# Attention stage of a two-layer hybrid backbone: weight splits in parts, low parts and LayerNorm sums on another engine, mean copied out of PSUM, other buffers for the MLP's input

## The chip, the cores and the metric

The kernel runs on one core of one Trainium2 chip. The metric is the device time of one execution in microseconds (us); the time of a kernel is the median of several executions. Engines are called PE (TensorE, with PEld for its weight loads), DVE (VectorE), ACT (ScalarE), POOL (GpSimd) and SP (SyncE, which here only issues DMAs).

## What is computed

Two post-norm layers over 1024 latent tokens and 256 context tokens of width 1024, all in float32. Layer 0 is retention and gated linear attention; layer 1, where the change lies, is windowed grouped-query attention in which latent queries also read all context keys. Cut to what matters here (the head axes, masks and modulation are in words):

```
h   = modulate(x)                               # shift and scale by SiLU(c)
q, k, v = split(h @ w_qkv)                      # 16 query heads, 4 KV heads, width 64, 2-D rotary on q and k
s   = q @ k.T / 8                               # keys: own block of 128 and its two neighbours (+-128), and 256 context keys
m   = max(s, sink[head]);  e = exp(s - m)
y   = (e @ v) / (sum(e) + exp(sink - m))        # learned sink logit for each head
x   = layer_norm(alpha * x + gate * (y @ w_out))
h   = modulate(x)
x   = layer_norm(alpha * x + gate2 * (square(relu(h @ w1)) @ w2))
```

`layer_norm` takes mean and variance over the 1024 channels of a token, then multiplies by g and adds b.

## The kernel before, in words

Activations lie transposed: channels on partitions (8 tiles of 128, `KT`), tokens on columns. A matmul in full precision is done in three: each float32 operand is split into a high part (a cast to the reduced type `F32R`) and a low part (the value less its high part), and `mm3` multiplies high with high, high with low and low with high. So every weight and every activation that enters such a matmul costs a cast and a subtraction on another engine.

The attention stage works on 32 groups: for each block n of 128 queries (0 to 7), each of four KV heads g, with the four query heads that share it. For a group:

- `scores(i)`, i from 0 to 3: the scores of one query head in a PSUM tile `pS` (two of them in turn), their maximum (L1400, DVE), the exponent's bias (L1401, DVE), the exponential into a tile `E` (L1404, ACT; seven buffers of 640 columns under the tag "E").
- `dens()`: the denominators, and `dg` (L1417, POOL), four diagonal tiles that carry their reciprocals.
- `turn(kk)`, five for a block inside (four in the first and the last block): four PE transposes of `E` into a PSUM bank `pE` (two in turn, L65), copied to `Et` by ACT (L1429), for kk = 2 by DVE (L1427).
- `pv(kk)`: the product with the values into `pO`. `end()`: the denominators' product, `yf` (L1448, L1449, DVE), its high part `yh` (L1451, ACT) and its low part `yl` (L1452, DVE).
- `qt`, the queries, come by two DMAs of POOL's queue (L1380) for every second group; two such tiles are used in turn.

The code weaves the groups: the scores of the next group are issued between the transposes of the present one. Into this weave it hangs, in small steps, the work on tokens whose attention is done, 256 at a time:

- `w_load` and `w_prep` bring one 128x1024 tile of the output weight for each group from the seventh on: DMA, high part by ACT (L1333), low part by `en` (L1334), which is POOL, but DVE for four of the last eight tiles.
- `residual` runs `w_out_steps`: for each of 8 output tiles 24 matmuls into the single PSUM bank `pW`, in two halves, then gate and addition (L758, DVE). The last residual has no group beside it and takes the two `pE` banks. Two of the residuals end with `make_h`, which makes the MLP's input from 256 tokens that are normalised already: `hf` by ACT (L378), its high part by DVE (L259), its low part by DVE and POOL in turn (L260, the list `los`). Here `hf` lies in the tag "ln_q", with one buffer.
- `norm` runs `layer_norm_steps` with `pe_sums` False: the eight channel tiles are added on DVE (L701, L703) into `sm` (named `ln_s` in rows), one matmul with ones turns that sum into the mean in `pW`, DVE subtracts it from PSUM (L712, 512 columns at a time), ACT squares (L714, tag "ln_q", one buffer), DVE adds the squares (L721), a second matmul gives the variance, then square root, reciprocal (L725), multiplication (L730, DVE) and g, b (L736, POOL). Three of these LayerNorms lie in the stage and what follows it; a fourth is made by other code on PE.

Behind the last group the last residual's remaining tiles and the third LayerNorm run by themselves, and then the MLP begins: its first matmuls (`k`, then squared ReLU from L1046 on) need `hf` split, its weights are split by L251 (ACT) and L252 (POOL).

What sets the order: PE's instructions in the groups are chained in the order of the code (`TE.kept`). On the other engines the scheduler of the framework sets the order at build time; each engine then takes its instructions strictly in that order. POOL's queue holds its arithmetic and its DMAs in one order.

Of the kernel before, what the change touches and what calls it, by code (L numbers as in the profile page):

```python
# [34 lines left out]
def backbone(ctx: ExitStack, tc: tile.TileContext, xT, cin, wmod, bmod, lng, lnb, w1, w2,  # L35
# [330 lines left out]

    def make_h(src, l, idx, j, hh, hl, tp, tag, nb=1, hi_eng=None):
        for _ in h_steps(src, l, idx, j, hh, hl, tp, tag, nb, hi_eng):
            pass

    def h_steps(src, l, idx, j, hh, hl, tp, tag, nb=1, hi_eng=None, los=(V, G)):

        n = src.shape[2]
        for k2 in range(KT // 2):
            tmp = tp.tile([P, 2, 256], F32, tag=tag, name=nm("hf"), bufs=nb)
            for i in range(2):
# [298 lines left out]

    def layer_norm_steps(acc, l, s, tp, ts, tq, nb, pe_sums, pL, qn=1024, tail=None):

# [20 lines left out]
        if pe_sums:  # L698
            part(pp, acc, 0, 4)
        else:  # L700
            V.tensor_tensor(sm[:, 0, :], acc[:, 0, :], acc[:, 1, :], ALU.add)  # L701
            for k in range(2, KT):
                V.tensor_tensor(sm[:, 0, :], sm[:, 0, :], acc[:, k, :], ALU.add)  # L703
                if k == 4:
                    yield
        yield
        pm = mean(pp, 0)
        pp = pL() if pe_sums else None
        st_ = qn // n
        for k0 in range(0, KT, st_):  # L710
# [4 lines left out]
            if pe_sums:  # L715
                part(pp, sq, k0 // 2, (k0 + st_) // 2)
            else:
                for i in range(st_):
                    if k0 + i == 0:
                        continue  # L720
                    V.tensor_tensor(sm[:, 1, :], sq[:, 0, :] if k0 + i == 1 else sm[:, 1, :], sq[:, i, :], ALU.add)  # L721
            yield
# [581 lines left out]
    with pool(name="p2", bufs=1) as p2:  # L1304
# [24 lines left out]
        def w_prep():  # L1329
            if raws:  # L1330
                raw, en = raws.pop(0)
                both = wg.tile([P, 2, 1024], F32R, tag="w", name=nm("w"))
                S.copy(both[:, 0, :], raw)  # L1333
                en.tensor_tensor(both[:, 1, :], raw, both[:, 0, :].bitcast(F32), ALU.subtract)  # L1334
                ready.append((both[:, 0, :], both[:, 1, :]))

        def residual(y, t, ci):
# [8 lines left out]
            if t in (NT - 3, NT - 1):  # L1346
                make_h(accs[1][:, :, o0:o0 + 256], 1, 1, 0, *[y_[:, :, o0:o0 + 256] for y_ in yall], p2, "ln_q", 1)

        def norm(t, ci):

            o0 = (t - 1) * P - CH[ci][0]
            TE.kept = False
            for _ in layer_norm_steps(accs[ci][:, :, o0:o0 + 256], 1, 0, p2, "ln_s", "ln_q", 1, False, pW, 512):
                yield
# [6 lines left out]
        def group(n, g):  # L1361
# [80 lines left out]
            def end():  # L1442
# [8 lines left out]
                S.copy(ysl, yf)  # L1451
                V.tensor_tensor(yall[1][:, 2 * g:2 * g + 2, lt:lt + P], yf, ysl.bitcast(F32), ALU.subtract)  # L1452

# [180 lines left out]
```

## Time and profile before

| | us |
|---|---|
| three executions | 3015.12, 3013.77, 3008.65; median 3013.77 |
| the profiled execution, its own time | 3020.45 |
| its span in the trace | 3018.6 |
| attention stage in the trace (groups) | 1847 to 2230 |
| last residual, LayerNorm, MLP's first input | 2222 to 2282 |

The mean granted clock of PE in the profiled execution is 0.979. In the rows a group of instructions reads: line, engine, operation, output<-input, partitions x elements, xcount | busy time in us, mean ns of one | idle time of the engine ahead of them, and what ended it. A row of the timeline reads: start in us, duration in us, engine, line, operation, tiles, and in brackets how long the engine was idle ahead of it and what released it. A row of waits reads: engine, tile and line that waited, what released it; us in all, number, longest.

### The profile page before, as it was taken

The page shows a single profiled execution, that of the slowest core. Times are in us where ns is not written, and L with a number is a line of the kernel's source. Part 1 is how long each engine was busy: PE and PEld are TensorE (multiplying, and loading weights), DVE is VectorE, ACT ScalarE, POOL GpSimd, SP SyncE. Part 2 cuts the span into 40 slices and gives each one's busy share as a digit, 9 for nine tenths or more (in the row PEclk, how much of TensorE's full clock was granted, in tenths as well). Part 3 has the DMA queues.
Part 4 walks back from the last instruction along what each step waited for, and adds up shares of the span by engine and source line. Part 5 has one row for each costly group of instructions (what it writes and reads, how often), then busy time and mean ns, then how long its engine had stood idle before and what let it go on. Part 6 is the DMA issues. An engine that isn't in the chain of part 4 may idle for free. (4 is left out here: it accounts for less than half of the span.)

```text
span 3018.6 us, 42215 instructions
## 1 busy us (share of the span) xinstructions
PE 2863.4 (95%) x17204; PEld 2403.4 (80%) x17204; DVE 1662.4 (55%) x2709; ACT 978.9 (32%) x1628; POOL 808.1 (27%) x610
## 2 busy tenths in 40 slices
PE   7989998999999999999999999898888999999997
PEld 4866788888888888888888777677677888888886
DVE  3754477777755544445434645677775343433345
ACT  4433344444221211111112623555553221122113
POOL 3120145545211111111111511333353222122111
PEclk9999999999999999999999999999999999999999
DMA  7377575663221221222200483221221111111111
GB/s 254 112 233 243 183 263 187 203 203 109 67 73 57 81 70 60 77 68 76 70 29 8 134 223 92 66 88 58 78 98 36 56 56 42 43 56 53 37 37 57
DMA packets 168353, 304.44 MB, mean 101 GB/s; under 512 B 13504, under 2 KB 98752, under 8 KB 167648
## 3 DMA queue, kind: packets, MB, share of 16 engines
q1 hardware_dynamic: 149744, 272.91, 27.7%
q0 software_dynamic: 6480, 16.26, 2.1%
q10 hardware_dynamic: 11936, 12.59, 1.5%
q8 instruction: 135, 2.21, 0.3%
q14 instruction: 58, 0.48, 0.0%
HBM read 257.67 MB, written 44.04 MB: 100 GB/s over the span
## 5 line engine op out<-in xcount | busy, mean ns | idle before, releaser
L252 POOL TENSOR_TENSOR w<-raw,w 128x1024 fp32r<-128x1024 f32 x182 | 439.4, 2423 | 1518.2 <-ACT w L251 1457.9
L62 PE MATMUL k<-hh,w 128*128 128x256 f32 (+1 forms) x3264 | 824.6, 338 | 5.3 <-DVE hh L259 3.4
L62 PE MATMUL k<-uh,w 128*128 128x512 f32 (+1 forms) x2816 | 764.4, 352 | 8.1 <-DVE acc L1064 7.7
L1064 DVE SCALAR_TENSOR_TENSOR acc<-k,gta,acc 128x512 f32<-128x512 f32 (+1 forms) x704 | 440.8, 648 | 565.7 <-PE k L62 564.0
L62 PEld LDWEIGHTS k<-hh,w 128*128 128x128 f32 x3264 | 567.6, 191 | 83.0 <-issue 12.9
L62 PEld LDWEIGHTS k<-uh,w 128*128 128x128 f32 x2816 | 501.4, 189 | 89.2 <-DVE acc L1064 15.4
L62 PE MATMUL k<-hl,w 128*128 128x256 f32 (+1 forms) x1632 | 553.1, 339 | 5.8 <-POOL hl L260 4.5
L62 PE MATMUL k<-ul,w 128*128 128x512 f32 (+1 forms) x1408 | 494.8, 351 | 0.0
L251 ACT CAST w<-raw 128x1024 fp32r<-128x1024 f32 x228 | 235.8, 1047 | 694.2 <-PE k L62 471.5
L62 PEld LDWEIGHTS k<-hl,w 128*128 128x128 f32 x1632 | 311.4, 191 | 45.4 <-POOL hl L260 5.9
L62 PEld LDWEIGHTS k<-ul,w 128*128 128x128 f32 x1408 | 266.1, 189 | 36.5 <-issue 1.2
L62 PE MATMUL k<-yh,w 128*128 128x256 f32 (+1 forms) x1088 | 271.9, 336 | 21.2 <-DVE acc L758 11.2
L1046 ACT ACTIVATE r<-k 128x512 f32<-128x512 f32 (+1 forms) x176 | 90.7, 516 | 613.1 <-PE k L62 610.9
L62 PEld LDWEIGHTS k<-yh,w 128*128 128x128 f32 x1088 | 192.6, 196 | 42.8 <-DVE acc L758 12.6
L181 DVE SCALAR_TENSOR_TENSOR k<-raw,cs,k 128x256 f32<-128x256 f32 (+1 forms) x168 | 96.5, 574 | 159.5 <-DMA raw<-in_wmod 157.4
L62 PE MATMUL k<-yl,w 128*128 128x256 f32 (+1 forms) x544 | 181.5, 334 | 0.0
L1049 DVE TENSOR_TENSOR r<-r 128x1024 f32<-128x1024 f32 (+1 forms) x88 | 110.6, 1257 | 72.0 <-ACT uh L1048 71.8
L62 PE MATMUL pS<-kall,qt 128*128 128x256 f32 (+1 forms) x512 | 124.5, 355 | 13.8 <-ACT E L1404 13.3
L736 POOL TENSOR_SCALAR acc<-acc,lg_t,lb_t 128x256 f32<-128x256 f32 x124 | 102.3, 839 | 103.0 <-DVE acc L730 56.8
L1404 ACT ACTIVATE E<-pS,sm 128x640 f32<-128x640 f32 (+1 forms) x128 | 98.7, 771 | 77.1 <-DVE sm L1401 75.0
L1400 DVE TENSOR_REDUCE sm<-pS 128x1 f32<-128x640 f32 (+1 forms) x128 | 100.4, 786 | 36.1 <-PE pS L62 33.5
L65 PE MATMUL pE<-ident,E 128*128 128x128 f32 x608 | 96.5, 284 | 21.1 <-DVE Et L1427 20.1
(279 smaller groups left out, 3862.9 us busy)
## 6 DMA issues: line engine op xcount, KB each, us to landing
raw<-in_w SPq DMA_DIRECT2D x128, 512.0 KB, 3.3
raw<-in_wo SPq DMA_DIRECT2D x72, 512.0 KB, 3.4
raw<-in_wmod SPq DMA_DIRECT2D x128, 256.0 KB, 2.7
raw<-in_wfm SPq DMA_DIRECT2D x48, 512.0 KB, 5.2
raw<-in_wmod SPq DMA_DIRECT2D x32, 512.0 KB, 4.4
kt<-kd SPq DMA_DIRECT2D x20, 512.0 KB, 5.5
qt<-qT POOLq DMA_DIRECT2D x32, 256.0 KB, 3.0
qT<-qT ACTq DMA_DIRECT2D x30, 256.0 KB, 3.2
```

What stands on the lines that cost most here:

```text
L62: return self.put(nc.tensor.matmul(*a, **kw))
L65: return self.put(nc.tensor.transpose(*a, **kw))
L181: V.scalar_tensor_tensor(dst, src, cs[:, k + a, j:j + 1], dst, op0=ALU.mult, op1=ALU.add)
L251: S.copy(hi, raw)
L252: (eng or G).tensor_tensor(lo, raw, hi.bitcast(F32), ALU.subtract)
L736: G.tensor_scalar(acc[:, k, :], acc[:, k, :], lg_t[:, l, s, k:k + 1], lb_t[:, l, s, k:k + 1], op0=ALU.mult, op1=ALU.add)
L1046: S.activation(rf[:, i, :n], pts[i][:, :n], AF.Relu)
L1049: V.tensor_tensor(rf[:, :, :n], rf[:, :, :n], rf[:, :, :n], ALU.mult)
L1064: V.scalar_tensor_tensor(a_, pt[:, :n], gta[:, l, 1, m, cj(ci):cj(ci) + 1], a_, op0=ALU.mult, op1=ALU.add)
L1400: V.tensor_reduce(sm_[:, 0, i:i + 1], sall, AX.X, ALU.max)
L1404: S.activation(E_[:, :256 + L], sall, AF.Exp, scale=0.125, bias=sm_[:, 1, i:i + 1], accum_out=sm_[:, 3, i:i + 1])
```

## The change

It has five parts. (1) POOL's low part of an output weight is made by four instructions of 256 columns and no longer by one of 1024; DVE's four stay whole. (2) The low part `yl` of the attention's output goes from DVE to POOL. (3) The sums of the three LayerNorms in the stage (seven additions for the mean, seven for the squares) go from DVE to POOL. (4) In these LayerNorms ACT copies the mean from PSUM to `sm`, and DVE subtracts it from there. (5) The MLP's input `hf` at the end of two residuals uses the tag "E" (seven buffers, 512 of 640 columns) and no longer "ln_q" (one), and all its low parts are made by DVE.

```diff
-    def make_h(src, l, idx, j, hh, hl, tp, tag, nb=1, hi_eng=None):
-        for _ in h_steps(src, l, idx, j, hh, hl, tp, tag, nb, hi_eng):
+    def make_h(src, l, idx, j, hh, hl, tp, tag, nb=1, hi_eng=None, los=(V, G)):
+        for _ in h_steps(src, l, idx, j, hh, hl, tp, tag, nb, hi_eng, los):
...
-            tmp = tp.tile([P, 2, 256], F32, tag=tag, name=nm("hf"), bufs=nb)
+            if tag == "E":
+                tmp = tp.tile([P, 640], F32, tag="E", name=nm("hf"), bufs=7)[:, 0:512].rearrange("p (a n) -> p a n", a=2)
+            else:
+                tmp = tp.tile([P, 2, 256], F32, tag=tag, name=nm("hf"), bufs=nb)
...
-            V.tensor_tensor(sm[:, 0, :], acc[:, 0, :], acc[:, 1, :], ALU.add)
+            adder.tensor_tensor(sm[:, 0, :], acc[:, 0, :], acc[:, 1, :], ALU.add)
             for k in range(2, KT):
-                V.tensor_tensor(sm[:, 0, :], sm[:, 0, :], acc[:, k, :], ALU.add)
+                adder.tensor_tensor(sm[:, 0, :], sm[:, 0, :], acc[:, k, :], ALU.add)
...
         pm = mean(pp, 0)
+        if adder is G:
+            S.copy(sm[:, 0, :], pm[:, :n])
+            pm = sm[:, 0, :]
...
-                    V.tensor_tensor(sm[:, 1, :], sq[:, 0, :] if k0 + i == 1 else sm[:, 1, :], sq[:, i, :], ALU.add)
+                    adder.tensor_tensor(sm[:, 1, :], sq[:, 0, :] if k0 + i == 1 else sm[:, 1, :], sq[:, i, :], ALU.add)
...
-                en.tensor_tensor(both[:, 1, :], raw, both[:, 0, :].bitcast(F32), ALU.subtract)
+                for o in range(0, 1024, 256 if en is G else 1024):
+                    sl = slice(o, o + 256 if en is G else 1024)
+                    en.tensor_tensor(both[:, 1, sl], raw[:, sl], both[:, 0, sl].bitcast(F32), ALU.subtract)
...
-                make_h(accs[1][:, :, o0:o0 + 256], 1, 1, 0, *[y_[:, :, o0:o0 + 256] for y_ in yall], p2, "ln_q", 1)
+                make_h(accs[1][:, :, o0:o0 + 256], 1, 1, 0, *[y_[:, :, o0:o0 + 256] for y_ in yall], p2, "E", 7, None, (V, V))
...
-            for _ in layer_norm_steps(accs[ci][:, :, o0:o0 + 256], 1, 0, p2, "ln_s", "ln_q", 1, False, pW, 512):
+            for _ in layer_norm_steps(accs[ci][:, :, o0:o0 + 256], 1, 0, p2, "ln_s", "ln_q", 1, False, pW, 512, adder=G):
...
-                V.tensor_tensor(yall[1][:, 2 * g:2 * g + 2, lt:lt + P], yf, ysl.bitcast(F32), ALU.subtract)
+                G.tensor_tensor(yall[1][:, 2 * g:2 * g + 2, lt:lt + P], yf, ysl.bitcast(F32), ALU.subtract)
```

Lines after the change are a few higher: L1334 becomes L1342, L1452 L1460, L1400 L1408, L1427 L1435, L703 L706, L712 L718, L721 L727, L378 L381. The order of PE and of SP in the rest of the program is the same.

**A group in the middle of the stage.** POOL's order, before: the diagonals `dg` of a group, a weight's low part, the queries' DMAs, the next group's `dg` and weight, and `dg` of the group after it.

```order
L1417 TENSOR_SCALAR dg_16547<-ident,sm_16454 128x128 x4
L1334 TENSOR_TENSOR w_16654<-raw_16431,w_16654 128x1024
L1380 DMA qt_16960<-qT_0_14271 128x512 x2
L1417 TENSOR_SCALAR dg_16681<-ident,sm_16559 128x128 x4
L1334 TENSOR_TENSOR w_16788<-raw_16541,w_16788 128x1024
```

POOL's order at the same place, after:

```order
L1425 TENSOR_SCALAR dg_16553<-ident,sm_16457 128x128 x4
L1342 TENSOR_TENSOR w_16660<-raw_16434,w_16660 128x256 x2
L1460 TENSOR_TENSOR yl<-yf_16542,yh 128x2x128
L1342 TENSOR_TENSOR w_16660<-raw_16434,w_16660 128x256 x2
L1388 DMA qt_16975<-qT_0_14271 128x512 x2
L1425 TENSOR_SCALAR dg_16690<-ident,sm_16565 128x128 x4
L1342 TENSOR_TENSOR w_16797<-raw_16547,w_16797 128x256 x2
L1460 TENSOR_TENSOR yl<-yf_16679,yh 128x2x128
L1342 TENSOR_TENSOR w_16797<-raw_16547,w_16797 128x256 x2
L704 TENSOR_TENSOR ln_s_17774<-acc_2330_16592 128x256
```

Each weight is in four parts, `yl` of the group ahead stands between the second and the third, the DMAs stand behind all five, and a LayerNorm's first sum (L704) has come in at the end of a group.

DVE's order at that place, before, from `yf` on: maximum (L1400) and bias (L1401) of each query head of the next group, with `yl` and the copy of `Et` between them.

```order
L1449 TENSOR_TENSOR yf_16536<-yf_16536,pO_2318_16523 128x256
L1400 TENSOR_REDUCE sm_16559<-pS_2325_16560 128x1
L1401 TENSOR_SCALAR sm_16559<-sm_16559,nsnk 128x1
L1452 TENSOR_TENSOR yl<-yf_16536,yh 128x2x128
L1400 TENSOR_REDUCE sm_16559<-pS_2328_16576 128x1
L1401 TENSOR_SCALAR sm_16559<-sm_16559,nsnk 128x1
L1427 COPY Et_16557<-pE_2332_16602 128x512
L1400 TENSOR_REDUCE sm_16559<-pS_2333_16608 128x1
L1401 TENSOR_SCALAR sm_16559<-sm_16559,nsnk 128x1
```

DVE's order there, after:

```order
L1457 TENSOR_TENSOR yf_16542<-yf_16542,pO_2318_16529 128x256
L1408 TENSOR_REDUCE sm_16565<-pS_2325_16566 128x1
L1409 TENSOR_SCALAR sm_16565<-sm_16565,nsnk 128x1
L1408 TENSOR_REDUCE sm_16565<-pS_2328_16582 128x1
L1409 TENSOR_SCALAR sm_16565<-sm_16565,nsnk 128x1
L1435 COPY Et_16563<-pE_2332_16608 128x512
L1408 TENSOR_REDUCE sm_16565<-pS_2333_16614 128x1
L1409 TENSOR_SCALAR sm_16565<-sm_16565,nsnk 128x1
```

`yl` is gone from between the first bias and the second maximum; nothing else has moved.

**A group with a LayerNorm's squares.** ACT's order, before (`ln_q` the squares, `w` a weight's high part, `E` an exponential):

```order
L714 ACTIVATE ln_q_18017<-acc_2330_16586 128x512
L1451 CAST yh<-yf_18009 128x2x128
L1429 COPY Et_18036<-pE_2582_18054 128x512
L1333 CAST w_18135<-raw_17883 128x1024
L714 ACTIVATE ln_q_18157<-acc_2330_16586 128x512
L1404 ACTIVATE E_18052,sm_18043<-pS_2580_18044,sm_18043 128x640
L1404 ACTIVATE E_18068,sm_18043<-pS_2583_18060,sm_18043 128x640
L714 ACTIVATE ln_q_18293<-acc_2330_16586 128x512
L714 ACTIVATE ln_q_18432<-acc_2330_16586 128x512
L1429 COPY Et_18036<-pE_2589_18099 128x512
L1429 COPY Et_18110<-pE_2590_18105 128x512
L1404 ACTIVATE E_18097,sm_18043<-pS_2587_18089,sm_18043 128x640
```

Behind these comes the last exponential. ACT's order there, after:

```order
L720 ACTIVATE ln_q_18057<-acc_2330_16592 128x512
L1437 COPY Et_18076<-pE_2582_18094 128x512
L1339 CAST w_18175<-raw_17919 128x1024
L720 ACTIVATE ln_q_18200<-acc_2330_16592 128x512
L1412 ACTIVATE E_18092,sm_18083<-pS_2580_18084,sm_18083 128x640
L1412 ACTIVATE E_18108,sm_18083<-pS_2583_18100,sm_18083 128x640
L720 ACTIVATE ln_q_18339<-acc_2330_16592 128x512
L1437 COPY Et_18076<-pE_2589_18139 128x512
L1437 COPY Et_18150<-pE_2590_18145 128x512
L1412 ACTIVATE E_18137,sm_18083<-pS_2587_18129,sm_18083 128x640
L720 ACTIVATE ln_q_18481<-acc_2330_16592 128x512
L1412 ACTIVATE E_18160,sm_18083<-pS_2592_18152,sm_18083 128x640
```

The copy of the mean (L712) stands three rows ahead of these; the third square stands ahead of the copies as before, and the fourth now stands between the last two exponentials.

**The last group.** ACT's order, before, from the last exponential on; then the square root of the second LayerNorm (another table is loaded for it) and the last group's copies.

```order
L1404 ACTIVATE E_19614,sm_19544<-pS_2845_19606,sm_19544 128x512
L1412 ACTIVATE sm_19544<-sm_19544 128x4
L724 ACT_TABLE_LOAD
L724 ACTIVATE ln_s_18851<-pW_2850_19648,eps_t 128x256
L1451 CAST yh<-yf_19643 128x2x128
L1429 COPY Et_19668<-pE_2853_19663 128x512
L1429 COPY Et_19668<-pE_2855_19670 128x512
```

ACT's order there, after:

```order
L1412 ACTIVATE E_19688,sm_19618<-pS_2845_19680,sm_19618 128x512
L1420 ACTIVATE sm_19618<-sm_19618 128x4
L381 ACTIVATE hf_19815<-acc_2330_16592,mod,osc 128x256 x2
L381 ACTIVATE hf_19820<-acc_2330_16592,mod,osc 128x256 x2
L381 ACTIVATE hf_19825<-acc_2330_16592,mod,osc 128x256
L730 ACT_TABLE_LOAD
L730 ACTIVATE ln_s_18909<-pW_2850_19725,eps_t 128x256
L1459 CAST yh<-yf_19720 128x2x128
L1437 COPY Et_19745<-pE_2853_19740 128x512
L1437 COPY Et_19745<-pE_2855_19747 128x512
```

Five instructions of the MLP's input (`hf`) now stand ahead of the table load and of the last group's copies; before, the first of them stood ten rows further down.

More of the change, by code (lines that the diff above doesn't have):

```diff
@@ L674, in layer_norm, with layer_norm_steps @@
             pass
-    def layer_norm_steps(acc, l, s, tp, ts, tq, nb, pe_sums, pL, qn=1024, tail=None):
+    def layer_norm_steps(acc, l, s, tp, ts, tq, nb, pe_sums, pL, qn=1024, tail=None, adder=V):
         n = acc.shape[2]
```

## Prediction

> **What bounds the kernel.** I read the page first (TensorE against the span), then TensorE's list of waits over the stage that the change touches, then four stretches of it, then the rows behind each wait.
>
> ```profile
> span 3018.6 us, 42215 instructions
> PE 2863.4 (95%) x17204; PEld 2403.4 (80%) x17204; DVE 1662.4 (55%) x2709; ACT 978.9 (32%) x1628; POOL 808.1 (27%) x610
> ```
>
> TensorE (PE) sets the end; what it does not wait for cannot be won. The change alters the attention stage (1847 to 2230) and the first steps of the MLP behind it. TensorE's waits there, by what ended them (us in all, times, longest):
>
> ```profile
> PE pE L65 <- DVE Et L1427: 20.1, 19, 1.1
> PE pS L62 <- ACT E L1404: 10.4, 10, 2.8
> PE pW L62 <- DVE acc L712: 10.1, 2, 5.4
> PE k L62 <- ACT r L1046: 10.0, 1, 10.0
> PE pE L62 <- DVE acc L758: 6.6, 2, 5.1
> ```
>
> These 57.2 us, under 2% of the span, are nearly all there is to win. Four groups: a normal one, one with a LayerNorm's squares (two such), one with a LayerNorm's end. Behind each window stand its length, busy us of PE, PEld, DVE, ACT, POOL, the granted clock, the DMA share and GB/s:
>
> ```profile
> 2053.00:2065.10 12.10, 11.04 (x90) 8.94 (x88) 8.82 (x16) 6.75 (x15) 4.94 (x7) 1.00 0.30 87
> 2065.10:2084.10 19.00, 13.60 (x92) 11.28 (x90) 13.40 (x27) 9.13 (x19) 3.76 (x5) 0.82 0.10 35
> 2120.40:2136.30 15.90, 13.11 (x92) 10.75 (x90) 14.49 (x25) 8.89 (x17) 9.90 (x14) 0.89 0.31 100
> 2172.60:2189.90 17.30, 12.61 (x92) 10.86 (x90) 12.41 (x27) 9.72 (x21) 3.77 (x5) 0.90 0.09 32
> ```
>
> A normal group has 12.10 - 11.04 = 1.06 us without TensorE. Its rows:
>
> ```profile
> 2056.83 0.60 PE L65 MATMUL pE<-ident,E 128*128 128x128 f32 x4
> 2055.34 2.39 POOL L1334 TENSOR_TENSOR w<-raw,w 128x1024 fp32r<-128x1024 f32 x1 [0.68 <-ACT w L1333]
> 2055.59 2.42 DVE L1452 TENSOR_TENSOR yl<-yf,yh 128x256 fp32r<-128x256 f32 x1
> 2057.94 0.81 DVE L1400 TENSOR_REDUCE sm<-pS 128x1 f32<-128x640 f32 x1
> 2058.91 0.68 DVE L1427 COPY Et<-pE 128x512 f32<-128x512 f32 x1
> 2059.65 0.66 PE L65 MATMUL pE<-ident,E 128*128 128x128 f32 x4 [1.06 <-DVE Et L1427]
> ```
>
> VectorE's yl (L1452) starts 0.25 us after GpSimd's 1024-column subtraction and ends with it: 2.42 us. Behind it stand a maximum (L1400) and the copy (L1427) that frees the PSUM bank for the fifth transposes. So the wait is made by yl being held. Alone, before the weights start, yl takes 0.42; an L1401, whose operands are one column wide, ran inside a 1024-column subtraction in 0.21; and in the last block the held yl is back ahead of L1401:
>
> ```profile
> 1865.28 0.42 DVE L1452 TENSOR_TENSOR yl<-yf,yh 128x256 fp32r<-128x256 f32 x1
> 1865.61 0.21 DVE L1401 TENSOR_SCALAR sm<-sm,nsnk 128x1 f32<-128x1 f32 x1
> 1866.74 0.50 PE L62 MATMUL pS<-kall,qt 128*128 128x256 f32 x2 [0.63 <-ACT E L1404]
> ...
> 1907.91 2.36 POOL L1334 TENSOR_TENSOR w<-raw,w 128x1024 fp32r<-128x1024 f32 x1 [0.69 <-ACT w L1333]
> 1908.29 0.21 DVE L1401 TENSOR_SCALAR sm<-sm,nsnk 128x1 f32<-128x1 f32 x1
> ...
> 2192.87 2.04 DVE L1452 TENSOR_TENSOR yl<-yf,yh 128x256 fp32r<-128x256 f32 x1
> 2217.36 0.50 PE L62 MATMUL pS<-kall,qt 128*128 128x256 f32 x2 [1.05 <-ACT E L1404]
> ```
>
> The rows that price the rest (count | busy us, mean ns):
>
> ```profile
> L1334 POOL TENSOR_TENSOR w<-raw,w 128x1024 fp32r<-128x1024 f32 x28 | 67.8, 2422 | 24.7 <-ACT w L1333 24.6
> L260 POOL TENSOR_TENSOR yl<-hf,yh 128x512 fp32r<-128x512 f32 x4 | 5.2, 1302 | 6.5 <-DVE yh L259 6.5
> L1452 DVE TENSOR_TENSOR yl<-yf,yh 128x256 fp32r<-128x256 f32 x30 | 57.0, 1900 | 0.6
> L721 DVE TENSOR_TENSOR ln_s<-ln_s,ln_q 128x256 f32<-128x256 f32 x18 | 14.5, 804 | 3.4 <-ACT ln_q L714 3.2
> L736 POOL TENSOR_SCALAR acc<-acc,lg_t,lb_t 128x256 f32<-128x256 f32 x24 | 19.7, 834 | 3.6 <-DVE acc L730 3.6
> L1451 ACT CAST yh<-yf 128x256 fp32r<-128x256 f32 x30 | 12.2, 407 | 2.3 <-DVE yf L1449 2.3
> 2053.24 1.42 POOL L1417 TENSOR_SCALAR dg<-ident,sm 128x128 f32<-128x128 f32 x4 [7.60 <-PE pO L62]
> 2061.33 1.14 POOL L1380 DMA_DIRECT2D qt<-qT  x2 [3.60 <-PE pS L62]
> ```
>
> **A GpSimd instruction of 256 columns** is not in the stage. From 512 and 1024 columns (1302, 2422 ns) the slope is 2.19 ns a column and the fixed part 0.18 us, so I take 0.74 us; bounds 0.61 (a quarter of 2422) and 1.30 (the 512-column row). Four parts are 2.97 us where one was 2.42.
>
> **Normal groups (yl moved, weight split in parts).** VectorE loses 2.42 us at 2055.59. The second maximum then starts when the first one's bias is done, the copy L1427 right after its transposes (56.83 + 0.60 = 57.43), done by 57.43 + 0.68 = 58.1; TensorE wants the bank at 59.65 - 1.06 = 58.59. The wait goes, 19 x 1.06 = 20.1. Next late would be the exponentials, which move forward with the maxima; I find none that bites. GpSimd then issues per group dg 1.42, four parts and yl, 5 x 0.74 = 3.70, every second group two qt DMAs 1.14, sometimes one sum 0.74: at most 7.0 of 11.0 us. The order puts yl between the second and third part, so it waits for ACT's yh (0.41 behind the cast) and holds two parts, used a group later: nothing. The qt DMAs stand behind all five, and now go out when TensorE frees qt (3.60 idle ahead of them before): 3.70 against 2.39 + 3.60 = 5.99 from the part's start, so on time; at the bound of 1.30 the five are 6.5, and qt would go out 0.5 late.
>
> The Trainium skill speaks against this move: "Perfetto Trace Analysis", section "Optimizing Scalar/DVE Operations", says GpSimd and VectorE share a read port, so that moving work between them might not help. The 2.42 us hold agrees that they do. What stays on VectorE in a normal group reads PSUM or a few columns, as the L1401 at 1908.29 that was not held, so by that page too the 20.1 go here.
>
> **Early groups (no weights yet).** yl's 0.42 lies ahead of the bias L1401 that the exponential waits for: five waits (0.63, 0.63, 0.85 three times) each lose about 0.41, 2.0 us. Ends 0 and 3.5.
>
> **Last block (n=7).** Three waits of 0.82, 0.84 and 1.05 (the last is above) come from a held yl of 2.0 to 2.3 ahead of L1401: 2.7 us.
>
> **The two LayerNorm groups.** The waits and the tail's, row by row:
>
> ```profile
> 2073.53 0.55 PE L62 MATMUL pW<-yh,w 128*128 128x256 f32 x1 [5.40 <-DVE acc L712]
> 2081.20 0.79 ACT L1404 ACTIVATE E<-pS,sm 128x640 f32<-128x640 f32 x1 [0.46 <-DVE sm L1401]
> 2128.08 0.44 PE L62 MATMUL pS<-kall,qt 128*128 128x384 f32 x1 [2.79 <-ACT E L1404]
> 2243.75 0.58 PE L62 MATMUL pE<-yh,w 128*128 128x256 f32 x1 [5.05 <-DVE acc L758]
> 2261.74 7.77 POOL L252 TENSOR_TENSOR w<-raw,w 128x1024 fp32r<-128x1024 f32 x3 [3.67 <-ACT w L251]
> 2275.05 1.26 POOL L260 TENSOR_TENSOR yl<-hf,yh 128x512 fp32r<-128x512 f32 x1
> 2276.35 1.09 ACT L378 ACTIVATE hf<-acc,mod,osc 128x256 f32<-128x256 f32 x2 [7.92 <-POOL yl L260]
> 2282.09 0.58 PE L62 MATMUL k<-yh,w 128*128 128x256 f32 x1 [10.00 <-ACT r L1046]
> ```
>
> TensorE waits 5.40 for pW's one bank, held until the last subtraction of the mean (L712). With the mean copied by ACT (0.41, as L1451) the bank is free near 2066.4, and this wait goes. What is late next is ACT: in its new order the third square stands ahead of the third exponential and the fourth square ahead of the fourth, and each square waits for its one ln_q buffer, that is for GpSimd's sums. GpSimd has dg to 2066.8, yl and the first sum to about 2068.9, four parts (2.97) to 2071.9, and only then two sums to 2073.4. Third square 0.64, two copies of Et 1.07, third exponential 0.8: 2075.9; the next two sums are done by then; fourth square, fourth exponential: 2077.4. Before, the fourth exponential ended at 2081.99 and the group at 2084.10, 2.1 us later; so now 2079.5, a group of 14.4 and not 19.0. The second such group goes the same way, 13.0 and not 17.3. Gain 4.6 + 4.3 = 8.9; ends 0 (the sums pace all as before) and 7.6 + 5.9 (TensorE's busy 11.4 alone).
>
> In the first of these windows the clock is 0.82. "TensorE: Matmul & The Clock Gate", part 1, of the Trainium skill has it that a clock dropped in idleness needs about 3.4 us of work to rise; the row agrees. By that page closing the 5.40 would bring about 1.7 more; I leave that out.
>
> **The group with the LayerNorm's end (15.9).** The 2.79 wait there is for exponentials behind yl and L730 on VectorE; without yl about 2.8 go. But GpSimd now holds there dg, yl, four parts, eight L736 (8 x 0.83), seven sums (5.2), dg and two parts, yl and two parts: some 20 us against a group of 13, so the next qt goes out late by 2 to 5 us, of which 1.6 to 3 reach TensorE. Net +1; ends -3 and +5.
>
> **The tail.** ACT issues five of the MLP's inputs (hf, 5 x 0.55) ahead of the last group's copies, about -1.6. GpSimd's chain of eight L736 (6.7), two weights' parts (5.9), yl (0.7) and seven sums (5.2) is 18.5 us; from the end of the last weight before it (2229.8 in the new course) the last LayerNorm's mean comes near 2248, between 2246 (L736 not held) and 2254 (its sums held by VectorE), and TensorE waits there instead of for 5.05. Seven buffers for hf take away the ring of one that a GpSimd yl (2275.05, behind three L252 of 2.42 us) ended so late: the first MLP step starts at 2276 to 2280 and not 2282.09, and its low parts on VectorE cost 2 x 0.83. Net +4; ends -3 (sums later than inputs) and +17 (both waits gone).
>
> **Sum.** 20.1 + 2.0 + 2.7 + 8.9 + 1 + 4 = 38.7. The profiled execution took 3020.45 us (span 3018.6), 6.7 above the median of the three runs, 3013.77; 3020.45 - 38.7 = 2981.7, and the same 6.7 lower: 2975.
>
> **Rivals.** (a) Only the held yl is won. The mean now lies in SBUF, so L712 takes two SBUF inputs and is held by GpSimd's sums as yl was by the weight; in LayerNorm groups and tail the hold only changes sides. For it: L721's 804 ns against 0.42 unheld. Against it: pW's bank is free whatever VectorE does. Gain 20.1 + 2.0 + 2.7 = 24.8: 2989. Chance 0.22. The Trainium skill, "SBUF — State Buffer", section "🔬 SBUF: two separate sides", has this rule: a VectorE operation with two SBUF inputs and a GpSimd operation exclude each other for the whole instruction.
> (b) All waits go but some 2 us of ramp, tail too: 57.2 - 2 = 55, 2959. For it: none of the waits is for TensorE itself; against it: the walk above finds GpSimd late twice. Chance 0.14.
> (c) Slower: GpSimd becomes the bound of every group. From (12.10 - 1.42 - 0.57) / 5 = 2.0 us for a 256-column instruction its queue is longer than the group; at 2.42 each (a fixed price that does not shrink with columns) five are 12.1 us, a group 15 to 16, and 26 groups lose 3.7 each: 96 us, 3110. The 512-column row at 1302 speaks against it. Chance 0.04.
> (d) No change: the bank's wait is replaced by one of the same size for an exponential or qt, and the tail gives back the rest: 3014. The 3.60 us that the qt DMAs idle now speak against it. Chance 0.05.
>
> **How the numbers follow.** My sum has 0.55; its own range is 2964 to 2986 from the ends of the LayerNorm groups and the tail. With (a) to 2998 and (b) down to 2952, what is left out is (c), (d) and some edges, under 2 in 10: 2952 to 2998. 0.2% of the time, 6 us, is what a measurement can tell from no change. Faster 0.55 + 0.22 + 0.14 = 0.91; same 0.05; slower 0.04.
>
> **What would show it.** Right: no wait of the fifth transposes for L1427 (19 gone), normal groups of 11.0 to 11.2 us, yl on GpSimd 0.7 to 0.8 us, the 5.40 gone, hf without 7.92 of idle time. Wrong: 256-column instructions above 1.5 us, qt landing after TensorE asks for it, a wait for exponentials of about 1 us in each normal group, or a mean matmul after 2254.

## The result, and the profile after

The changed kernel takes 2977.46 us (median of four, 2970.71 to 2984.53) against 3012.78 before: a ratio of 0.9884, 95% interval 0.9856 to 0.9913. Run again later it took 2973.53, a ratio of 0.9853 (0.9830 to 0.9875). The forecast was 2975, and 2952 to 2998 for the range. The profiled execution took 2984.53, 35.9 less than the profiled one of before. One execution of the kernel with `yl` alone and one of the kernel with `hf` alone ran at a granted clock of 0.747 and took 3539 and 3549 us; the times below leave them out.

The page of the changed kernel, and its longest TensorE waits from 1840 to 2300 us (us in all, times, longest):

```profile
span 2982.6 us, 42297 instructions
PE 2855.2 (96%) x17204; PEld 2399.9 (80%) x17204; DVE 1600.2 (54%) x2639; ACT 979.7 (33%) x1631; POOL 881.9 (30%) x764
```

```profile
PE pS L62 <- ACT E L1412: 8.4, 13, 1.5
PE pE L62 <- POOL yl L1460: 5.3, 1, 5.3
PE k L62 <- ACT r L1052: 4.3, 1, 4.3
PE pW L62 <- POOL ln_s L706: 3.8, 1, 3.8
PE pW L62 <- POOL yl L1460: 2.4, 1, 2.4
```

The 19 waits for VectorE's copy of `Et` are gone (one new wait of 0.5 us stands in the second squares group), and so is `pW` waiting for VectorE. The waits of the scores for an exponential, 8.4 us here, were 13.3 us in the same stretch of the kernel before; the 10.4 of the prediction's row is for a stretch without the first groups. VectorE lost 62 us of work and GpSimd gained 74; two of the waits that are left now name GpSimd's `yl`, one its sums. The kinds of group in the order of the prediction (normal, LayerNorm's squares, LayerNorm's end, then the group behind that end, which the prediction's rows don't have, squares again), with length, busy us of PE, PEld, DVE, ACT, POOL, clock, DMA share and GB/s:

```profile
2029.00:2039.80 10.80, 10.80 (x92) 8.93 (x90) 6.68 (x15) 6.79 (x15) 4.93 (x9) 1.00 0.23 75
2050.50:2062.80 12.30, 11.64 (x94) 9.39 (x92) 8.93 (x17) 7.69 (x17) 10.54 (x14) 1.00 0.23 76
2095.80:2108.60 12.80, 11.57 (x92) 9.35 (x90) 10.60 (x18) 8.92 (x18) 9.88 (x16) 1.00 0.48 146
2108.60:2122.10 13.50, 11.06 (x90) 9.00 (x88) 7.21 (x16) 6.78 (x15) 12.49 (x21) 1.00 0.05 12
2143.80:2156.00 12.20, 11.48 (x92) 9.21 (x90) 8.84 (x17) 7.45 (x16) 10.47 (x14) 1.00 0.19 63
```

TensorE now fills a normal group: 10.80 busy of 10.80, where it was 11.04 of 12.10. The timeline of that group shows why (GpSimd, then VectorE's copy, then the fifth transposes):

```profile
2031.74 1.43 POOL L1342 TENSOR_TENSOR w<-raw,w 128x256 fp32r<-128x256 f32 x2 [0.64 <-ACT w L1339]
2033.13 0.72 POOL L1460 TENSOR_TENSOR yl<-yf,yh 128x256 fp32r<-128x256 f32 x1
2033.87 0.69 DVE L1435 COPY Et<-pE 128x512 f32<-128x512 f32 x1 [0.81 <-PE pE L65]
2034.39 1.03 PE L65 MATMUL pE<-ident,E 128*128 128x128 f32 x8
```

VectorE now idles 0.81 us until TensorE has the transposes ready, copies them at once, and the next transposes follow without a bracket: eight in one row.

To compare runs I take two lengths from each trace: from the first group's last product to the last group's (rows of `pO<-dg`; their distances are the lengths of the groups), and from there to the end of the span. For before and after:

```profile
1862.84 0.60 PE L62 MATMUL pO<-dg,ones_c 128*64 128x256 f32 x4
2227.35 0.60 PE L62 MATMUL pO<-dg,ones_c 128*64 128x256 f32 x4
```

```profile
1871.74 0.60 PE L62 MATMUL pO<-dg,ones_c 128*64 128x256 f32 x4
2191.77 0.60 PE L62 MATMUL pO<-dg,ones_c 128*64 128x256 f32 x4
```

The groups took 364.5 and then 320.0, the rest 791.2 and 790.8. Ahead of the first row, where both kernels have the same instructions, the later trace is 8.9 longer, so that the spans differ by 36.0 only. Over the fourteen profiles of this study that row lay between 1853.4 and 1871.7. TensorE's busy time ahead of it lay between 1774 and 1788 us for the same matmuls, and the mean granted clock between 0.979 and 0.988, lower as a rule where the row came later; so most of this spread goes with the clock, and what sets the clock there is open. It is why the sums of the two lengths are compared below and not the spans.

### The profile page after: what moved, and what is told of

The parts are those of the page before. It is cut to its first block, busy times and chain, and to the rows that moved or that the text cites. A ratio compares the mean times of both kernels' runs of the same rounds, so it can differ in the third digit from the quotient of the medians.

```text
span 2982.6 us, 42297 instructions
## 1 busy us (share of the span) xinstructions
PE 2855.2 (96%) x17204; PEld 2399.9 (80%) x17204; DVE 1600.2 (54%) x2639; ACT 979.7 (33%) x1631; POOL 881.9 (30%) x764
## 5 line engine op out<-in xcount | busy, mean ns | idle before, releaser
L252 POOL TENSOR_TENSOR w<-raw,w 128x1024 fp32r<-128x1024 f32 x182 | 441.7, 2435 | 1517.8 <-ACT w L251 1473.2
L742 POOL TENSOR_SCALAR acc<-acc,lg_t,lb_t 128x256 f32<-128x256 f32 x124 | 103.3, 845 | 104.8 <-DVE acc L736 58.4
L1408 DVE TENSOR_REDUCE sm<-pS 128x1 f32<-128x640 f32 (+1 forms) x128 | 101.0, 791 | 33.9 <-PE pS L62 31.3
L62 PEld LDWEIGHTS k<-yl,w 128*128 128x128 f32 x544 | 106.1, 195 | 9.1
```

Of the source, the lines that this page charges most:

```text
L62: return self.put(nc.tensor.matmul(*a, **kw))
L252: (eng or G).tensor_tensor(lo, raw, hi.bitcast(F32), ALU.subtract)
L742: G.tensor_scalar(acc[:, k, :], acc[:, k, :], lg_t[:, l, s, k:k + 1], lb_t[:, l, s, k:k + 1], op0=ALU.mult, op1=ALU.add)
L1408: V.tensor_reduce(sm_[:, 0, i:i + 1], sall, AX.X, ALU.max)
```

## The experiments

Groups, rest and their sum are the two lengths above, in us, of one profile each. Each ratio is to the kernel before as it ran beside it on the same chip, not to the 3012.78 of the first row. A single profile can be off by some us through the clock alone: the one of before by 4.3, as the next section shows.

| kernel | groups | rest | sum | normal group | the two squares groups | time, ratio to before (interval) |
|---|---|---|---|---|---|---|
| before | 364.5 | 791.2 | 1155.7 | 12.10 | 18.97, 17.31 | 3012.78 |
| yl alone | 326.0 | 794.6 | 1120.5 | 10.82 | 19.63, 15.14 | 2986.01, 0.9892 (0.9872 to 0.9913) |
| parts alone | 326.6 | 791.0 | 1117.6 | 10.82 | 16.83, 16.38 | 2983.39, 0.9881 (0.9856 to 0.9906) |
| LayerNorm alone | 352.6 | 795.9 | 1148.4 | 12.10 | 13.13, 10.93 | 3008.43, 0.9969 (0.9948 to 0.9990) |
| hf alone | 361.8 | 789.7 | 1151.5 | 12.10 | 19.46, 18.23 | 3011.19, 0.9994 (0.9979 to 1.0010) |
| all but yl | 318.0 | 792.5 | 1110.5 | 10.82 | 12.15, 10.92 | 2968.64, 0.9851 (0.9834 to 0.9869) |
| all but parts | 325.3 | 789.2 | 1114.5 | 10.82 | 13.70, 14.93 | 2975.28, 0.9862 (0.9845 to 0.9880) |
| all but hf | 319.7 | 798.7 | 1118.4 | 10.82 | 12.23, 12.25 | 2979.07, 0.9883 (0.9867 to 0.9899) |
| last on VectorE | 317.4 | 795.6 | 1112.9 | 10.82 | 12.23, 12.24 | 2973.77, 0.9866 (0.9852 to 0.9881) |
| copy alone | 350.6 | 794.9 | 1145.5 | 12.10 | 12.89, 14.85 | 3006.87, one time |
| sums alone | 355.9 | 793.4 | 1149.3 | 12.10 | 15.80, 15.26 | 3005.71, one time |
| all but yl, half of L736 on ACT | 317.9 | 788.2 | 1106.1 | 10.82 | 12.14, 10.93 | 2971.44, 0.9851 (0.9836 to 0.9866) |
| the change | 320.0 | 790.8 | 1110.8 | 10.82 | 12.23, 12.25 | 2977.46, 0.9884 (0.9856 to 0.9913) |
| the change again | 321.5 | 790.6 | 1112.1 | 10.82 | 12.24, 12.25 | 2973.53, 0.9853 (0.9830 to 0.9875) |

### Each part alone

```diff
-                V.tensor_tensor(yall[1][:, 2 * g:2 * g + 2, lt:lt + P], yf, ysl.bitcast(F32), ALU.subtract)
+                G.tensor_tensor(yall[1][:, 2 * g:2 * g + 2, lt:lt + P], yf, ysl.bitcast(F32), ALU.subtract)
```

> Only the low part yl goes to GpSimd; the weight's low part stays one instruction of 1024 columns. Theory A (the loss in the groups was yl held on VectorE by that instruction): VectorE has nothing to be held in a normal group, so its groups fall from 12.10 to about 10.8 us, the two groups with weights but without output matmuls (12.76 and 13.68 before) to 9.1, the last block's lose about 3 in all; the LayerNorm groups stay at 19.0 and 17.3. Gain about 31: 2982, between 2976 and 2988. Rival B (the split is what helps; behind a whole weight GpSimd is late with yl or the queries' DMAs): the groups stay above 11.5 and the time above 2998.

Theory A held: every normal group at 10.82, the two with weights but without output matmuls at 9.1, the time in the upper part of its range; the second squares group fell to 15.14, which it had not expected, and the rest is 3.3 longer. The 1024-column instruction in one piece does no harm to `yl` behind it, which GpSimd does in 730 ns.

```diff
-                en.tensor_tensor(both[:, 1, :], raw, both[:, 0, :].bitcast(F32), ALU.subtract)
+                for o in range(0, 1024, 256 if en is G else 1024):
+                    sl = slice(o, o + 256 if en is G else 1024)
+                    en.tensor_tensor(both[:, 1, sl], raw[:, sl], both[:, 0, sl].bitcast(F32), ALU.subtract)
```

> Only the weight's low part is made in four instructions of 256 columns; yl stays on VectorE. Theory A (VectorE gets in between two of GpSimd's instructions): yl is held by one part at most, 0.42 + 0.75 us, the bank is free at 58.4 where it is wanted at 58.6, normal groups of 10.8 to 11.2 us, gain 25 to 31: 2982 to 2988. Rival B (queued parts keep the other engine out until the last): yl takes 2.9 or more, normal groups 12.4 to 12.8, 3020 to 3030.

Theory A again, and this is what the prediction had not seen: with `yl` left on VectorE the normal groups fall to the same 10.82. In the trace of this run GpSimd's four parts and VectorE's `yl` lie side by side, and the last row prices `yl` over all groups:

```profile
2041.10 3.00 POOL L1336 TENSOR_TENSOR w<-raw,w 128x256 fp32r<-128x256 f32 x4 [0.69 <-ACT w L1333]
...
2041.36 0.77 DVE L1454 TENSOR_TENSOR yl<-yf,yh 128x256 fp32r<-128x256 f32 x1
...
L1454 DVE TENSOR_TENSOR yl<-yf,yh 128x256 fp32r<-128x256 f32 x32 | 20.7, 645 | 0.5
```

`yl` starts 0.26 us into the first part and ends 1.03 after the parts' start, 2 us ahead of the end of the fourth, though the parts follow one another without idle time. So it is held by one instruction and then let in, and GpSimd waits in its turn: the second of the four took 925 ns, the others 729 to 737. The mean of `yl` is 645 ns and not 1900. By the Trainium skill ("SBUF — State Buffer", section "🔬 SBUF: two separate sides") the loser of the shared pair is blocked for the whole instruction; these rows agree, and add that it does not have to wait for the queue.

```diff
-            for _ in layer_norm_steps(accs[ci][:, :, o0:o0 + 256], 1, 0, p2, "ln_s", "ln_q", 1, False, pW, 512):
+            for _ in layer_norm_steps(accs[ci][:, :, o0:o0 + 256], 1, 0, p2, "ln_s", "ln_q", 1, False, pW, 512, adder=G, cp=True):   # cp: ACT copies the mean
```

> Only the LayerNorm sums go to GpSimd and the mean is copied by ACT; yl and whole weights as before. Theory A (the 5.40 us were pW's bank): the two LayerNorm groups fall from 19.0 and 17.3 to 12 to 15 us, gain 5 to 12: 3001 to 3008. Rival B (the hold only changes sides, since the subtraction of the mean now reads two operands in SBUF): the groups stay above 16 us, gain or loss under 4: 3009 to 3017.

Theory A for the two groups (13.13 and 10.93), and the time is 0.4 past the slow end of its range, since most of it is given back. The group behind the second squares group takes 16.47 in place of 10.57: TensorE waits three times there, 3.5 us in all, for a copy and two exponentials of ACT, and the clock is 0.79. ACT came late to the first two, as one of its squares and the first `hf` had waited 2.3 and 1.7 us for GpSimd's sums; the third stands behind a held `yl` (2.38 us). Behind the last group TensorE waits 9.6 us for GpSimd's sums, and the rest is 4.7 longer. With the 4.3 us of the profile of before taken off, this part alone is worth 3.0 us of the sum.

```diff
-                make_h(accs[1][:, :, o0:o0 + 256], 1, 1, 0, *[y_[:, :, o0:o0 + 256] for y_ in yall], p2, "ln_q", 1)
+                make_h(accs[1][:, :, o0:o0 + 256], 1, 1, 0, *[y_[:, :, o0:o0 + 256] for y_ in yall], p2, "E", 7, None, (V, V))
```

> Only the MLP's input goes through the seven E buffers with all its low parts on VectorE. Theory A (the wait of 10.0 us at the MLP's first step came from the ring of one): it falls to 4 or less, less 1.6 for five instructions ahead of the last group's copies: gain 4 to 8, 3005 to 3009; groups unchanged at 12.10. Rival B (the step is paced by GpSimd's weights and the LayerNorm before it): gain under 2, 3011 to 3015.

Theory B. The wait of 10.0 falls to 1.2 as A has it, but the rest is only 1.5 shorter: a wait of 5.6 us for VectorE's sums of squares takes most of its place, and the last group is 1.3 longer. The 4.2 us in the table's sum are the 4.3 of the profile of before.

### The whole change less one part

The kernel is the changed one, and the edit is taken back:

```diff
-                G.tensor_tensor(yall[1][:, 2 * g:2 * g + 2, lt:lt + P], yf, ysl.bitcast(F32), ALU.subtract)
+                V.tensor_tensor(yall[1][:, 2 * g:2 * g + 2, lt:lt + P], yf, ysl.bitcast(F32), ALU.subtract)
```

> The whole change, but yl stays on VectorE. Theory A (moving yl and splitting the weight cure the same wait, either is enough): normal groups of 10.82 us, the first seven groups together 1.5 to 2 longer, the group after the LayerNorm's end 2.4 shorter, since its output matmul waited for yl behind GpSimd's sums: the groups from the first to the last 319 to 322 us (320.0 with yl moved), time 2973 to 2979. Rival B (with the sums on GpSimd too, yl on VectorE is held again): normal groups of 11.3 or more, groups together over 328, 2985 or more.

Theory A: normal groups of 10.82 with `yl` on VectorE, 320.0 in the whole change against 318.0 here, and the group behind the LayerNorm's end at 10.82 in place of 13.52. The groups are 1 us below their range, since the second squares group fell to 10.92 too, which had not been expected; the time is 4 below its own.

```diff
-                for o in range(0, 1024, 256 if en is G else 1024):
-                    sl = slice(o, o + 256 if en is G else 1024)
-                    en.tensor_tensor(both[:, 1, sl], raw[:, sl], both[:, 0, sl].bitcast(F32), ALU.subtract)
+                en.tensor_tensor(both[:, 1, :], raw, both[:, 0, :].bitcast(F32), ALU.subtract)
```

> The whole change, but the weight's low part is one instruction of 1024 columns. Theory A: normal groups of 10.82 us and LayerNorm groups of 12 to 13.5, since 2.42 in one piece is no longer than four parts; groups together 318 to 324 us, 2973 to 2981. Rival B (a whole weight holds VectorE's subtraction of the mean, which now has two operands in SBUF): LayerNorm groups of 15 or more, groups together over 326, 2984 or more.

Between the two. The time and the normal groups are those of A; the groups' sum, 325.3, lies past A's end. The squares groups are 1.5 and 2.7 longer than with parts, and the group behind the LayerNorm's end takes 15.74, at a clock of 0.89. Here the parts do earn something: 3.7 us of the sum of both lengths against the first profile of the change, 2.4 against the second, which had the low clock in that group too.

```diff
-                make_h(..., p2, "E", 7, None, (V, V))
+                make_h(..., p2, "ln_q", 1)
```

> The whole change, but the MLP's input goes through one ln_q buffer as before. Theory A (five instructions ahead of the last group's copies cost 1.3, the ring of one costs 5 to 6 at the MLP's first step): last group 5.5 in place of 6.8, what follows the groups 5 to 7 us longer: 2980 to 2984. Rival B (as in the run of this part alone, what it gains at the first step is given back by GpSimd's work behind it): 2975 to 2979.

By the trace theory A: the last group 5.52 in place of 6.81, the rest 7.9 longer with a wait of 9.5 us at the MLP's first step. The time, 2979.07, lies at the border of the two. What gains nothing alone (the run of `hf` alone) gains 7.6 by the sums beside the other parts.

No run is the whole change less the LayerNorm part; what that part earns beside the others is not measured.

### Where TensorE still waits

```diff
-                G.tensor_tensor(yall[1][...], yf, ysl.bitcast(F32), ALU.subtract)
+                (V if g == 3 and n % 2 else G).tensor_tensor(yall[1][...], yf, ysl.bitcast(F32), ALU.subtract)
...
-            for _ in layer_norm_steps(..., adder=G):
+            for _ in layer_norm_steps(..., adder=G if t < 7 else V):   # the mean is copied for all three
```

> The whole change, but the yl of each group that ends 256 tokens and the sums of the third LayerNorm stay on VectorE (its mean is still copied). Theory A (where GpSimd has a queue, TensorE now waits 2.4 for yl in the group after the LayerNorm's end and 5.3 for the last yl, 3.8 for the sums): these three waits fall to 3 or less together, less what VectorE is held: gain of 5 to 9 on the changed kernel, 2969 to 2973. Rival B (these steps are paced by the weights and the LayerNorm's last multiplication on GpSimd whatever adds): under 2, 2975 to 2979.

A for one wait of the three, and B for the kernel: the sum, 1112.9, is 2.1 longer than the change's, and the time, 2973.77, can't be told from it. The group behind the LayerNorm's end falls from 13.52 to 10.82 and its wait is gone; behind the last group the two GpSimd waits turn into waits of 7.8 us (three) for VectorE's L764 and 4.9 for VectorE's sums, and the rest is 4.8 longer. There GpSimd's work holds VectorE: an addition of L727 takes 2.1 to 2.6 us beside a weight of the MLP (L252, 1024 columns, 2.3 to 2.4 us) and 0.42 without one. This change doesn't split L252.

```diff
         pm = mean(pp, 0)
+        S.copy(sm[:, 0, :], pm[:, :n])
+        pm = sm[:, 0, :]
```

> To the kernel before only the copy of the mean to SBUF by ACT is added; the sums stay on VectorE. Theory A (the 5.40 us were pW's bank, held until the last subtraction): the two LayerNorm groups fall from 19.0 and 17.3 to 12.5 to 14.5 us. Rival B (the chain of VectorE's sums and subtractions, held by the whole weight, paces the group in any case): they stay above 16. Either way the other groups are 12.10.

```diff
-            V.tensor_tensor(sm[:, 0, :], acc[:, 0, :], acc[:, 1, :], ALU.add)   # and the other sums
+            G.tensor_tensor(sm[:, 0, :], acc[:, 0, :], acc[:, 1, :], ALU.add)
```

> To the kernel before only the move of the LayerNorm sums to GpSimd is added; the mean is read from PSUM as before. Theory A (the bank is what TensorE waits for): VectorE reaches the last subtraction about 2 us sooner, since no sum of its own is held ahead of it, so the LayerNorm groups fall to 15.5 to 17.5 only. Rival B (the sums are what held everything): they fall to 13.5 or less, as with both.

The copy alone brings 12.89 and 14.85, the sums alone 15.80 and 15.27; A for both, but for the second of the copy's groups, 0.35 past its end, and the second of the sums' groups, 0.23 ahead of its end. In the waits of the run with the sums alone, TensorE still waits for the bank:

```profile
PE pW L62 <- DVE acc L715: 5.6, 2, 2.9
```

L715 is that kernel's L712. With the copy alone no such row is left. So in the first squares group the bank was nearly all of it: the copy alone does as well as both (13.13). In the second neither alone is enough (10.93 with both), but there both together give the gain back in the next group (16.47, with the copy alone 9.57). From the first group to the last the copy alone gains 9.6 us, when the 4.3 of the profile of before are taken off, and copy and sums together 7.6. That moving the sums earns anything beside the copy is not shown.

```diff
-                if tail is not None and k % 2 == 0:
+                if (half or tail is not None) and k % 2 == 0:      # half = t > 3; and yl on V
                     S.activation(acc[:, k, :], acc[:, k, :], AF.Identity, ...
```

> The whole change with yl left on VectorE, and in the second and third LayerNorm of the stage half of the multiplications by g (L736) on ACT instead of GpSimd. Theory A (GpSimd's queue behind the last group holds the third LayerNorm's sums: TensorE waits 5.8 and 3.1 us for them there): four L736 of 0.8 to 1.1 fewer in that queue, these waits together 3 to 4 us less, the rest behind the last group 788 to 790 (792.5 without); 2963 to 2967 where the version without it has 2968.6. Rival B (VectorE's holds or the weights' parts pace it): under 1 us, 2966 to 2972.

The rest is 788.2, as A has it, but not by its way: the two waits for GpSimd's sums are 5.1 and 3.0 where they were 5.8 and 3.1. That is 0.8 us of the 4.3 saved; the others were not traced to one step. The time lies outside A's range and in B's. By the trace this version is the shortest of all (1106.1); by its time, 2971.44, it can't be told from the change, 2973.53 beside it on the same chip.

> The changed kernel once more, beside the version with yl on VectorE. By the trace, from the first group to the end both take the same (1110.8 and 1110.5 us), so theory A: the medians lie within 0.25% of each other, 2966 to 2976 both, and what set them 9 us apart lies ahead of the first group. Rival B (leaving yl on VectorE is a gain of its own): this one is slower by 7 to 11 us again.

Theory A: 2973.53 (this is the changed kernel, no edit). That leaving `yl` on VectorE is a gain of its own is not shown; the two intervals are nearly the same. The version beside it on this chip was the one of the run above, with half of L736 on ACT too; the one with only `yl` on VectorE was not run again. In this profile the group behind the LayerNorm's end took 15.06 where it had taken 13.52, with the same wait but at a clock of 0.89 and not 1.00.

## Why the prediction was right, step by step

**The sum.** The two lengths fell by 1155.7 - 1110.8 = 44.9. Of that 4.3 belongs to the profile of before alone: the two groups with weights but without output matmuls took 12.76 and 13.68, where the same code took 11.07 and 11.08 in the run with hf alone. Their windows, of before and then of that run:

```profile
1905.10:1917.90 12.80, 10.40 (x68) 6.90 (x66) 8.20 (x17) 6.81 (x16) 4.91 (x7) 0.87 0.29 83
1917.90:1931.60 13.70, 11.74 (x68) 7.71 (x66) 8.21 (x15) 6.72 (x15) 4.10 (x6) 0.75 0.36 125
```

```profile
1894.00:1905.00 11.00, 8.60 (x68) 6.03 (x66) 7.79 (x16) 6.99 (x17) 3.90 (x6) 1.00 0.17 48
1905.00:1916.00 11.00, 8.59 (x66) 6.08 (x64) 8.13 (x16) 6.64 (x16) 5.12 (x8) 1.00 0.34 97
```

The clock is 0.87 and 0.75 in the one and 1.00 in the other. So the change is worth 40.6 by its first trace and 39.3 by its second; the forecast was 38.7, and the medians give 35.3 and 41.4 (2973.53 against 3014.93). That it came so close is in part luck. By the first trace the normal groups, the squares groups, the LayerNorm's end and the last block brought 7.7 us more than their terms, and the early groups and the tail 5.8 less.

**Normal groups: right, slightly small.** 1.06 was predicted for each and 1.28 came, since TensorE's busy time fell too, from 11.04 to 10.80: the fourth and fifth transposes, parted by the wait, took 0.60 and 0.66 us (at 2057.99 and 2059.65), and 1.03 in one row without it. The two without output matmuls gained 1.98 each (11.07 to 9.09), as they had waited for exponentials too. The reason given was half of it: `yl` was held, but not having it on VectorE is only one cure. Moving it and splitting what holds it gain 30.9 and 33.8 of the same 40 alone, and together not the sum.

**A 256-column instruction of GpSimd: right.** 0.74 was estimated. In groups of the changed kernel:

```profile
L1342 POOL TENSOR_TENSOR w<-raw,w 128x256 fp32r<-128x256 f32 x112 | 87.0, 800 | 12.1 <-ACT w L1339 12.0
L1460 POOL TENSOR_TENSOR yl<-yf,yh 128x256 fp32r<-128x256 f32 x32 | 23.4, 730 | 1.3 <-ACT yh L1459 1.3
```

That put an end to rival (c), which needed 2.0.

**Early groups: wrong, small.** 2.0 was predicted, 0.6 came (five groups, 42.23 to 41.60). The step that failed is that all of `yl`'s 0.42 was put on the path to the exponential. Counted from the first group's product, L1401 starts at 2.77 us before and at 2.55 after, 0.22 sooner, and the second maximum at 2.89 and 2.87, no sooner, as it waits for its scores. Before, one wait of 0.63 stood in such a group; after, two stand there:

```profile
1875.43 0.51 PE L62 MATMUL pS<-kall,qt 128*128 128x256 f32 x2 [0.42 <-ACT E L1412]
1876.97 0.50 PE L62 MATMUL pS<-kall,qt 128*128 128x256 f32 x2 [0.23 <-ACT E L1412]
```

The first exponential is sooner, and TensorE waits the difference at the second, which is not.

**Last block: right.** 2.7 predicted; its three full groups went from 31.98 to 28.93.

**Squares groups: gain right in kind, too small.** 8.9 predicted, 6.7 + 5.1 = 11.8 came, 0.6 of it lost again in the group behind the first. The step that failed is the end of the walk: it had the group's end follow its fourth exponential by 2.1 us. That exponential is the next group's; it holds up only the next group's transposes, by 0.4 us. It ends 13.6 us behind the row of `pO<-dg` that begins the group, where the walk had 12.8, and the group takes 12.2 all the same. What came is made of two things. The waits for the bank fell from 5.40 and 4.69 to waits of 0.66 and 0.50 for other rows, 8.9 in all, which the sum of the walk met by luck. And TensorE's busy time fell by 2.0 and 1.1 (13.60 to 11.64, 12.61 to 11.48) while the clock went from 0.82 and 0.90 to 1.00, which fits the term for the clock that the prediction left out. Rival (a), no gain here since the subtraction now reads two operands in SBUF, fell with it: 12.2 where it has 17 to 19. It is true that it is held: L718 takes 898 ns in the mean where L712 took 679.

**The LayerNorm's end: net right, mechanism wrong.** +1 predicted; 15.90 fell to 12.79 and the next group rose from 12.10 to 13.52, net +1.7. Of the wait of 2.79 in the first of them 1.23 is left; the busy time fell by 1.5 (13.11 to 11.57), at a clock of 1.00 and no longer 0.89. In the second trace of the change the net is +0.2, since the next group took 15.06. The late one is not the queries' DMAs but `yl`:

```profile
2110.83 4.81 POOL L706 TENSOR_TENSOR ln_s<-ln_s,acc 128x256 f32<-128x256 f32 x6
2117.00 1.41 POOL L1342 TENSOR_TENSOR w<-raw,w 128x256 fp32r<-128x256 f32 x2
2118.37 0.72 POOL L1460 TENSOR_TENSOR yl<-yf,yh 128x256 fp32r<-128x256 f32 x1
2119.14 0.39 PE L62 MATMUL pW<-yl,w 128*128 128x256 f32 x1 [2.44 <-POOL yl L1460]
```

GpSimd's queue of the sums, `dg` and two parts ends in this `yl`, which the next output matmul needs at once. The prediction had counted the queue and looked for the wrong reader of it.

**The tail: too good by 4 to 5.** +4 was predicted; the last group lost 0.8 and the rest gained 0.4. The places were right:

```profile
2202.20 0.58 PE L62 MATMUL pE<-yl,w 128*128 128x256 f32 x1 [5.32 <-POOL yl L1460]
2214.51 1.22 PE L62 MATMUL pW<-ln_s,ones_d 128*128 128x256 f32 x2 [3.77 <-POOL ln_s L706]
2243.62 0.39 PE L62 MATMUL k<-yh,w 128*128 128x256 f32 x1 [4.29 <-ACT r L1052]
```

On the clock of before (35.6 later, by the rows of the last group) the mean's matmul is at 2250.1 (predicted near 2248, 2246 to 2254) and the MLP's first step at 2279.2 (2276 to 2280). Missing from the sum was the 5.32 for the last `yl`: it stands behind four L742 and a weight's parts in GpSimd's queue, and the prediction had counted it there as 0.7 us of work and not as something that TensorE waits for. So the 5.05 for VectorE's addition, which the prediction had as gone, has only changed its name.

Rival (b), with all waits gone, had the tail's GpSimd queue against it and that is what remains: four of the five rows of waits shown above, 15.8 us, are for GpSimd or ACT in the tail and behind the LayerNorm's end. Rival (d) did not occur.

## What to carry to other kernels

Where an operation takes several times as long as elsewhere in the same trace, and ends with an instruction of another engine, suspect that it is held by it: look for both cures, moving the short one or cutting the long one, and test each alone, since either may bring all there is. Before moving work into an engine's queue, list what will stand behind it and who reads that at once; here the queue was counted well and its reader missed, twice. A PSUM bank that is read several times by a late engine is freed sooner by one copy. And count a gain in one group together with the group behind it, since a wait can move there.

## What the runs showed of the hardware that was not expected

- An instruction of VectorE that is held by GpSimd gets in between two of GpSimd's instructions that follow each other without idle time: `yl` took 0.77 us beside four parts of 3.00 in all, and 2.42 beside one instruction of 2.39. The part behind it took 925 ns and the other three 729 to 737.
- Whether idle time of the same kind lowers TensorE's clock is not the same from run to run. The two groups with weights but without output matmuls, their code unchanged, took 11.07 to 11.09 in three profiles, 11.08 and 12.77 in a fourth, and 12.76 and 13.68 in the one of before. The clock is 1.00 where they took 11.07 to 11.09 and 0.75 to 0.90 where they took longer, though no single wait of TensorE in them is above 1.07 us. 20 products took 2.38 us in the run with `hf` alone and 4.07 in the one of before:

```profile
1904.50 2.38 PE L62 MATMUL pO<-Et,v 128*64 128x256 f32 x20
```

```profile
1913.93 4.07 PE L62 MATMUL pO<-Et,v 128*64 128x256 f32 x20
```

The group behind the LayerNorm's end shows it again: 13.52 in one profile of the changed kernel and 15.06 in the other, with the same wait of 2.4 us, at clocks of 1.00 and 0.89. "TensorE: Matmul & The Clock Gate", part 1, of the Trainium skill has the clock set by how busy the engine was in a window of time; that a wait of this length sometimes lowers it and sometimes doesn't would fit a window that starts at any point, but no run here shows the window.
- The queries' DMAs of GpSimd's queue took longer from issue to landing in the changed kernel, 4.3 us in the median and 6.4 at most, against 3.0 and 3.9; no wait of TensorE for them is in the traces. With only `yl` or only the parts changed the median is 3.1 and 3.3, and with the whole change but `yl` or but the parts 3.3 and 3.1: it is longer only where GpSimd has both. Why is open.
